# A feed-forward stage with a written-out order on every engine

## The chip, the cores and the metric

The kernel runs on one core of one Trainium2 chip. Its time is the device time of one launch in microseconds (us), the median of three runs. Beside it stands one profiled execution, from which all rows below come. The engines are TensorE (PE), VectorE (DVE), ScalarE (ACT), GpSimd (POOL) and SyncE (SP); SP issues nearly all DMAs here. SBUF is the on-chip memory, PSUM the eight banks into which matmuls accumulate.

## The reference

One layer on x of 1024 positions by 1024 channels, float32: pre-norm, one input projection, a convolution branch and a stick-breaking attention branch, a gated merge, an output projection, a post-norm added to the residual; then a dense feed-forward with 2816 hidden columns, post-normed and added again. The change lies in the last three lines and in the norms around them:

```python
h = rmsnorm(x, norm_ffn_pre)
gu = jnp.einsum('bsd,df->bsf', h, w_ffn_up)
gate, up = jnp.split(gu, 2, axis=-1)
ff = jnp.einsum('bsf,fd->bsd', jax.nn.silu(gate) * up, w_ffn_down)
x = x + rmsnorm(ff, norm_ffn_post)
```

## The kernel before

All products are float32 from three matmuls: an operand is split into a high part `wh` (a rounded copy, ACT) and a low part `wl` (the rest, a subtraction on POOL or DVE), and `mm3` (L74) adds high×high (L77), high×low (L78) and low×high (L80).

The feed-forward takes 2×2 blocks with seven products in place of eight. In the up phase, block f of 22 (`up`, L894) runs products 1, 2, 6, 5, 7, 3, 4, each 12 matmuls of 128x512 into one PSUM bank. Their weights come from two DMAs, `rg` (gate half) and `ru` (up half). `rg` split gives products 1 and 2 (`prep_a`); two DVE sums of `ru` and `rg` (`s`, L863, L864) give products 5 and 6; two more in place of `rg` (L865, L866) give 7 and 3; half of `ru` gives 4. DVE and ACT turn the banks into u2, u3, c11, c12, c22 and two activations a1, a2; on odd blocks POOL makes four sums `sa` of them. All are stored to DRAM. Product 4 multiplies with T4, made on DVE from T2 and B21 (`make_t4`, L883).

Beside this, `weight_sums` (L838) makes sums of the down weights: a tile `q` is loaded, four DVE operations of 128x256 run in place (L841 to L844), and the result is stored. `jobs` (L1023) says at which block each of the 22 is written down.

The down phase is 42 steps, six for each of seven products, in the order 1, 6, 7, 5, 4, 2, 3. `ready(n)` (L1002) splits the step's two operands, `ra` with POOL and `rb` with DVE, three steps ahead; `cell` (L1012) runs the matmuls into four banks; `evacuate` (L1104) empties them, and for products 4 and 3 also normalises, adds x1 and stores (`finish`, L1097).

Between the output projection and the up phase, `post(tb)` (L688) makes the residual x1 and the normed tile `xr` for 128 rows, and `operands(tb)` (L728) transposes and splits it. The first products, 1 and 2 of blocks 0 to 2, need only half of the rows and run early (L805 to L812).

A scheduler orders the instructions of each engine by its own costs, apart from those that `keep_in_program_order` pins (one use, L723). A tile waits for the readers of what lay in its place before. An engine takes its instructions strictly one after the other: one that waits holds those behind it.

Of the kernel before, what the change touches and what calls it, by code (L numbers as in the profile page):

```python
# [15 lines left out]
P = 128  # L16
# [21 lines left out]
def layer_kernel(ctx, tc, x, vecs, dww, gains, ident_d, mask_d, wv, wi, wbr, wo, wu, wdq, wd, out):  # L38
# [649 lines left out]
    def post(tb):  # L688
# [77 lines left out]
    for tb in range(2):  # L766
        post(tb)
    for tb in range(2, NT):
        pos_[tb] = [bank("po"), bank("po")]
        if tb < NT - 1:  # L770
            for e in range(2):
                out_steps(tb, e, range(NK), pos_[tb][e])
        else:
            for d in range(NK):
                for e in range(2):
                    out_steps(tb, e, [d], pos_[tb][e])
        operands(tb - 2)
        post(tb)

# [18 lines left out]
    for f in range(2):  # L798
        fetch_gate(f)
        prep_a(f)  # L800
    raw2 = op_.tile([P, 1024], F32, name="rg2", tag="wh", bufs=6)
    SP.dma_start(out=raw2, in_=wu[2])
    w2 = split(raw2, op_, tag="w", bufs=6)
    ops[2] = {1: (w2, 0), 2: (w2, HALF)}
    early[0] = [bank("m1"), bank("m2")]  # L805
    prod(early[0][0], *ops[0][1], B11)
    operands(NT - 2)
    prod(early[0][1], *ops[0][2], B21)
    for f in (1, 2):
# [3 lines left out]
    pin[0] = True  # L813
    operands(NT - 1)
# [9 lines left out]
    fp.tile([P, 4, 256], F32, name="q0", tag="q", bufs=2)  # L824
# [34 lines left out]
    def prep_s12(f):  # L859
        rg, ru = rgs[f], rus[f]  # L860
        s12 = fp.tile([P, 1024], F32, name="s12", tag="s", bufs=1)
        s1, s2 = s12[:, 0:HALF], s12[:, HALF:1024]
        V.tensor_tensor(out=s1, in0=ru[:, 0:HALF], in1=ru[:, HALF:1024], op=ALU.add)  # L863
        V.tensor_tensor(out=s2, in0=s1, in1=rg[:, 0:HALF], op=ALU.subtract)  # L864
        V.tensor_tensor(out=rg[:, 0:HALF], in0=rg[:, 0:HALF], in1=ru[:, 0:HALF], op=ALU.subtract)  # L865
        V.tensor_tensor(out=rg[:, HALF:1024], in0=rg[:, HALF:1024], in1=s2, op=ALU.subtract)  # L866
        w = split(s12, fp)
        ops[f][5], ops[f][6] = (w, 0), (w, HALF)

    def prep_s34(f):  # L870
# [12 lines left out]
    def make_t4():  # L883
        for k in range(4):
# [7 lines left out]
    quads = {}  # L892

    def up(f, mid):  # L894
        if f not in early:
            early[f] = [bank("m1")]
            product(f, 1, early[f][0])
        if len(early[f]) == 1:
            early[f].append(bank("m2"))
            product(f, 2, early[f][1])  # L900
# [6 lines left out]
        last = f == NFB - 1  # L907
        p6, p5, p7, p3, p4 = [None] * 5

        def run(i):  # L910
            ps = bank(f"m{i}")
            product(f, i, ps)
            return ps

        if last:
            p5, p3 = run(5), run(3)
            mid(0)
        p6 = run(6)
        V.tensor_tensor(out=u2, in0=p6, in1=u2, op=ALU.add)
        if not last:  # L920
            mid(0)
            p5 = run(5)
        mid(1)
        p7 = run(7)
        u3 = ev("u3")
        V.tensor_tensor(out=u3, in0=p7, in1=u2, op=ALU.add)
        up2 = half_tile("c22", "c", 3)
        V.tensor_tensor(out=up2, in0=p5, in1=u3, op=ALU.add)
        V.tensor_tensor(out=u2, in0=p5, in1=u2, op=ALU.add)
        if not last:  # L930
            p3 = run(3)
# [270 lines left out]
```

## Time and profile before

| | us |
|---|---|
| median of 3 runs | 1479.9 (1479.01 to 1481.78) |
| the profiled execution, its own time | 1481.82 |
| its span | 1479.8 |

The span is the time from the first to the last instruction that the profiler saw; about 2 us of the execution's time lie outside it. Mean granted TensorE clock over the span: 0.975 of full speed. PE is busy for 1381.4 us of the span. The output projection ends and the feed-forward begins at about 787 us; the up phase runs to 1256 us, the down phase to 1472 us.

### The profile page before, as it was taken

The page shows a single profiled execution, that of the slowest core. Times are in us where ns is not written, and L with a number is a line of the kernel's source. Part 1 is how long each engine was busy: PE and PEld are TensorE (multiplying, and loading weights), DVE is VectorE, ACT ScalarE, POOL GpSimd, SP SyncE. Part 2 cuts the span into 40 slices and gives each one's busy share as a digit, 9 for nine tenths or more (in the row PEclk, how much of TensorE's full clock was granted, in tenths as well). Part 3 has the DMA queues.
Part 4 walks back from the last instruction along what each step waited for, and adds up shares of the span by engine and source line. Part 5 has one row for each costly group of instructions (what it writes and reads, how often), then busy time and mean ns, then how long its engine had stood idle before and what let it go on. Part 6 is the DMA issues. An engine that isn't in the chain of part 4 may idle for free.

```text
span 1479.8 us, 17335 instructions
## 1 busy us (share of the span) xinstructions
PE 1381.4 (93%) x6412; PEld 1131.8 (76%) x6412; DVE 1021.7 (69%) x1221; ACT 528.0 (36%) x863; POOL 619.9 (42%) x465
## 2 busy tenths in 40 slices
PE   6988998998999879999997899899999999999997
PEld 5866787877888667887786677677888888788886
DVE  6498878776999996235347997787666543754583
ACT  5466655553102105132324312222333223443441
POOL 2233323332315232323205555544666654554672
PEclk9999999999999989999999899999999999999999
DMA  6011001101111110213322266654333334976552
GB/s 219 23 28 37 22 23 32 41 29 36 50 43 51 43 43 22 64 43 122 127 87 100 91 206 228 238 195 156 107 114 110 106 100 146 321 277 199 197 186 85
DMA packets 62403, 160.97 MB, mean 109 GB/s; under 512 B 6384, under 2 KB 17904, under 8 KB 62320
## 3 DMA queue, kind: packets, MB, share of 16 engines
q1 hardware_dynamic: 62320, 159.88, 32.9%
q8 instruction: 50, 0.82, 0.2%
q14 instruction: 33, 0.27, 0.1%
HBM read 117.65 MB, written 40.11 MB: 107 GB/s over the span
## 4 chain that ended last, share of the span: by engine, by line
PE 60%; DVE 24%; issue 7%; DMA 3%; POOL 3%; ACT 2%; SPq 0%; DVEq 0%; POOLq 0%; ACTq 0%
DVE acc L453 11%; PE m L77 7%; PE m L78 7%; PE m L80 7%; PE md L77 4%; PE md L78 4%; PE md L80 4%; PE pg L77 2%; PE pg L78 2%; PE pg L80 2%; POOL wl L787 2%; DVE R L260 2%; PE po L670 1%; PE po L669 1%; PE po L668 1%
## 5 line engine op out<-in xcount | busy, mean ns | idle before, releaser
L71 POOL TENSOR_TENSOR wl<-wraw,wh 128x1024 fp32r<-128x1024 f32 (+1 forms) x58 | 139.9, 2418 | 251.4 <-ACT wh L70 146.6
L453 DVE SCALAR_TENSOR_TENSOR acc<-u,dw,acc 128x1024 f32<-128x1024 f32 x120 | 177.0, 1532 | 0.3
L77 PE MATMUL m<-hH,wh 128*128 128x512 f32 x352 | 139.5, 396 | 0.0
L78 PE MATMUL m<-hL,wh 128*128 128x512 f32 x352 | 138.9, 395 | 0.0
L1008 POOL TENSOR_TENSOR wl<-ra,wh 128x1024 fp32r<-128x1024 f32 (+1 forms) x42 | 101.4, 2417 | 85.5 <-ACT wh L1007 78.5
L77 PE MATMUL m<-t,wh 128*128 128x512 f32 x264 | 108.2, 410 | 23.2 <-ACT wh L786 16.5
L1008 DVE TENSOR_TENSOR wl<-rb,wh 128x1024 fp32r<-128x1024 f32 (+1 forms) x42 | 90.5, 2163 | 55.0 <-ACT wh L1007 43.6
L77 PE MATMUL md<-wh 128*128 128x512 f32 x308 | 120.6, 394 | 3.4 <-ACT wh L1007 3.4
L78 PE MATMUL md<-wl,wh 128*128 128x512 f32 x308 | 120.8, 392 | 0.0
L787 POOL TENSOR_TENSOR wl<-rg,wh 128x1024 fp32r<-128x1024 f32 x44 | 110.0, 2500 | 25.3 <-ACT wh L786 22.7
L70 ACT ACTIVATE wh<-wraw 128x1024 fp32r<-128x1024 f32 (+1 forms) x60 | 56.5, 944 | 144.6 <-PE pg L78 50.7
L78 PE MATMUL m<-t,wh 128*128 128x512 f32 x264 | 107.1, 406 | 0.0
L77 PE MATMUL pg<-hH,wh 128*128 128x512 f32 x256 | 101.2, 395 | 0.0
L78 PE MATMUL pg<-hL,wh 128*128 128x512 f32 x256 | 99.7, 389 | 0.0
L80 PE MATMUL md<-wh,wl 128*128 128x512 f32 x308 | 97.5, 390 | 0.0
L80 PE MATMUL m<-hH,wl 128*128 128x512 f32 x352 | 95.6, 393 | 0.0
L863 DVE TENSOR_TENSOR s<-ru 128x512 f32<-128x512 f32 x22 | 39.1, 1778 | 72.6 <-POOL wl L787 72.6
L77 PEld LDWEIGHTS m<-t,wh 128*128 128x128 f32 x264 | 51.4, 195 | 39.0 <-ACT wh L786 18.5
L1007 ACT ACTIVATE wh<-ra 128x1024 fp32r<-128x1024 f32 (+1 forms) x42 | 41.5, 989 | 109.8 <-issue 73.8
L261 POOL TENSOR_TENSOR R<-sg,R 128x512 f32<-128x512 f32 x32 | 46.7, 1461 | 81.0 <-DVE R L260 77.6
L787 POOL TENSOR_TENSOR wl<-ru,wh 128x512 fp32r<-128x512 f32 x22 | 30.5, 1385 | 114.8 <-ACT wh L786 114.6
L77 PEld LDWEIGHTS m<-hH,wh 128*128 128x128 f32 x352 | 66.6, 189 | 15.5
(224 smaller groups left out, 3559.9 us busy)
## 6 DMA issues: line engine op xcount, KB each, us to landing
ra<-act SPq DMA_DIRECT2D x35, 512.0 KB, 4.7
wraw<-in_wi SPq DMA_DIRECT2D x32, 512.0 KB, 3.6
rg<-in_wu SPq DMA_DIRECT2D x23, 512.0 KB, 3.6
ru<-in_wu SPq DMA_DIRECT2D x22, 512.0 KB, 4.1
q<-in_wdq SPq DMA_DIRECT2D x22, 512.0 KB, 4.0
wsum<-q SPq DMA_DIRECT2D x22, 512.0 KB, 2.9
act<-sa SPq DMA_DIRECT2D x44, 256.0 KB, 2.6
rb<-wsum SPq DMA_DIRECT2D x20, 512.0 KB, 4.3
```

Of the source, the lines that this page charges most:

```text
L70: A.activation(out=wh, in_=raw, func=AF.Copy)
L71: (sub or G).tensor_tensor(out=wl, in0=raw, in1=wh.bitcast(F32), op=ALU.subtract)
L77: PE.matmul(ps, lhsT=lh, rhs=rh, start=(first and j == 0), stop=False)
L78: PE.matmul(ps, lhsT=lh, rhs=rl, start=False, stop=False)
L80: PE.matmul(ps, lhsT=ll, rhs=rh, start=False, stop=(last and j == n - 1))
L260: V.tensor_tensor_scan(out=R[:, 4:4 + n][:, ::-1], data0=d, data1=d, initial=carry, op0=ALU.mult, op1=ALU.bypass)
L261: G.tensor_tensor(out=R[:, 4:4 + n], in0=sg[:, 0:n], in1=R[:, 4:4 + n], op=ALU.mult)
L453: V.scalar_tensor_tensor(out=acc, in0=u[:, kk:kk + S], scalar=dw[:, cb, kk:kk + 1], in1=acc, op0=ALU.mult, op1=ALU.add)
L787: (low or G).tensor_tensor(out=wl, in0=src, in1=wh.bitcast(F32), op=ALU.subtract)
L863: V.tensor_tensor(out=s1, in0=ru[:, 0:HALF], in1=ru[:, HALF:1024], op=ALU.add)
L1007: A.activation(out=h, in_=src, func=AF.Copy)
L1008: eng.tensor_tensor(out=l, in0=src, in1=h.bitcast(F32), op=ALU.subtract)
```

## The change

`post(tb)` now comes before `operands(tb - 2)`, and the last two x1 stores are issued by ACT. The first gate weights are fetched inside the loop over tb. All six early products stand together, with the last `operands` between the last two. The pool of the up phase, "upp", sets the places of the tags c, ev, q, ch, cl first, so that `ru` and `s` come to lie elsewhere. The weight sums and splits are cut into four functions. From the up loop to the end all five engines are wrapped in `Ordered`, which pins every instruction to the written order. `weight_sums(f)` stands once in each block. Block 0 runs products 3, 5, 6, 7, 4, with `make_t4` between, and the last block the same without it. The stores of the result go through `late` and `flush`.

```diff
@@ post
         V.tensor_tensor(out=x1, in0=x1, in1=xt, op=ALU.add)
-        SP.dma_start(out=x1d[tsl, :], in_=x1)
+        if tb < NT - 2:
+            SP.dma_start(out=x1d[tsl, :], in_=x1)
...
+        if tb >= NT - 2:
+            A.dma_start(out=x1d[tsl, :], in_=x1)
@@ before the up loop
+        post(tb)
         operands(tb - 2)
-        post(tb)
...
+        if NT - 4 < tb < NT - 1:
+            f = tb - NT + 3
+            fetch_gate(f)
+            prep_a(f)
+    raw2, wh2, wl2 = [op_.tile([P, 1024], dt, name=nm, tag="wh", bufs=6) for nm, dt in (("rg2", F32), ("wh2", F32R), ("wl2", F32R))]
...
+    for f in range(3):
         early[f] = [bank("m1"), bank("m2")]
         prod(early[f][0], *ops[f][1], B11)
+        if f == 2:
+            pin[0] = True
+            operands(NT - 1)
         prod(early[f][1], *ops[f][2], B21)
...
-    fp.tile([P, 4, 256], F32, name="q0", tag="q", bufs=2)
+    for tag, w, n in (("c", HALF, 3), ("ev", HALF, 3), ("q", 1024, 2), ("ch", HALF, 1), ("cl", HALF, 1)):
+        fp.tile([P, w], F32, name=f"{tag}0", tag=tag, bufs=n)
@@ up
+    class Ordered:
...
+        def __getattr__(self, nm):
+            fn = getattr(self.eng, nm)
+            return lambda *a, **k: tc.keep_in_program_order(fn(*a, **k))
...
+        if 2 < nf < NFB:
+            prep_a(nf)
         u2 = ev("u2")
         A.activation(out=u2, in_=p1, func=AF.Copy)
+        if more and f:
+            sums_12(nf)
...
+        if f == 0 or last:
+            run(3)
+            run(5)
+            if f == 0:
+                make_t4(range(4))
+                sums_12(nf)
+            run(6)
+            after_6()
+        else:
+            run(6)
+            after_6()
+            run(5)
+        weight_sums(f)
+        if more:
+            split_12(nf)
+        run(7)
...
+        if more:
+            sums_34(nf)
...
+        if more:
+            split_34(nf)
+        run(4)
+        if more:
+            prep_c(nf)
@@ the up loop
-    jobs = [[] for _ in range(NFB)]
-    for n in range(NFB):
-        jobs[min(1 + n if n < 10 else n, NFB - 2)].append(n)
...
+    PE, V, A, G, SP = [Ordered(e) for e in (PE, V, A, G, SP)]
     for f in range(NFB):
...
+        up(f)
@@ finish
-            SP.dma_start(out=out[tb * P:(tb + 1) * P, es], in_=parts[e])
+            late.append((out[tb * P:(tb + 1) * P, es], parts[e]))
```

What this does to the queues is shown at three places. In these rows L910 stands for every pinned instruction, since all are issued from that line.

The first is DVE at the start of the up phase, before the change: `da`, `db` and `t` are T4, `s` and `rg` the sums of block 0's weights.

```order
L886 TENSOR_TENSOR da<-t_5787,hH 128x512
L887 TENSOR_TENSOR db<-t_5787,hL 128x512
L886 TENSOR_TENSOR da<-t_5787,hH 128x512
L888 TENSOR_TENSOR da<-da,db 128x512
L887 TENSOR_TENSOR db<-t_5787,hL 128x512
L886 TENSOR_TENSOR da<-t_5787,hH 128x512
L863 TENSOR_TENSOR s_6717<-ru 128x512
L890 TENSOR_TENSOR t_6660<-da,t_6660 128x512
L864 TENSOR_TENSOR s_6717<-s_6717,rg 128x512
```

And after it, at the same place (`c_6742` is c11 of block 0):

```order
L867 TENSOR_TENSOR s_6721<-ru 128x512
L868 TENSOR_TENSOR s_6721<-s_6721,rg 128x512
L872 TENSOR_TENSOR rg<-rg,ru 128x512
L873 TENSOR_TENSOR rg<-rg,s_6721 128x512
L910 TENSOR_TENSOR c_6742<-m_6553,u_6740 128x512
L910 TENSOR_TENSOR da<-t_5787,hH 128x512
L910 TENSOR_TENSOR db<-t_5787,hL 128x512
```

The sums of block 0 moved ahead of T4. Further along the same queue T4 ends so (`s_6805` are the sums of block 1, `u_6740` is u2 of block 0, which empties its product 6):

```order
L910 TENSOR_TENSOR t_6660<-da,t_6660 128x512
L910 TENSOR_TENSOR s_6805<-ru 128x512
L910 TENSOR_TENSOR s_6805<-s_6805,rg 128x512
L910 TENSOR_TENSOR u_6740<-m_6808,u_6740 128x512
L910 TENSOR_TENSOR q<-q 128x256 x4
```

All 16 operations of T4 and the first two sums of block 1 now stand ahead of the operation that empties block 0's product 6, and one `weight_sums`, the four operations on `q`, behind it.

The second place is SP at the end of the output projection, before the change. Of the names, `x1d` is the store of the residual, `rg_6521` the gate weights of block 2, `ru` the up weights of blocks 0 and 1.

```order
L691 DMA xr<-in_x 128x1024
L802 DMA rg_6521<-in_wu 128x1024
L702 DMA x1d<-x_6395 128x1024
L702 DMA x1d<-x_6491 128x1024
L857 DMA ru<-in_wu 128x1024 x2
```

The two stores of x1 stand ahead of `ru`. After the change:

```order
L691 DMA xr<-in_x 128x1024
L806 DMA rg_6521<-in_wu 128x1024
L861 DMA ru<-in_wu 128x1024 x2
L840 DMA q<-in_wdq 128x1024
L910 DMA rg<-in_wu 128x1024
```

The two stores left SP's queue. The first `ru` now takes the place of `wl2`, the low part of block 2's gate weights, and so waits for the last matmul of block 2's product 2; before, it took a place that `xr` of the last 128 rows held.

The third is DVE at the end of the down phase's product 4, where `wl<-rb` is a split for a step to come, `du<-du,md` empties a bank, and the operations with `pr` and `x1r` finish a tile of the result. Before:

```order
L1118 TENSOR_TENSOR du_10001<-du_10001,md 128x512
L1118 TENSOR_TENSOR du_10002<-du_10002,md 128x512
L1008 TENSOR_TENSOR wl<-rb,wh 128x1024
L103 TENSOR_SCALAR pv<-ss_10013 128x1
L1118 TENSOR_TENSOR du_10003<-du_10003,md 128x512
L1101 SCALAR_TENSOR_TENSOR du_10001<-du_10001,pr,x1r 128x512
```

A split stands between the second and the third bank. After:

```order
L910 TENSOR_TENSOR du_10005<-du_10005,md 128x512
L910 TENSOR_SCALAR pv<-ss_10017 128x1
L910 SCALAR_TENSOR_TENSOR du_10005<-du_10005,pr,x1r 128x512
L910 SCALAR_TENSOR_TENSOR dc_10009<-dc_10009,pr,x1r 128x512
L910 TENSOR_TENSOR du_10006<-du_10006,md 128x512
L910 TENSOR_SCALAR pv<-ss_10018 128x1
```

The four tiles are now finished one after the other, and the next split stands behind the last of them (16 rows in all).

## Rows read from the trace of the kernel before

**Rows 1.** The page: busy us, share of the span, instructions.

```profile
PE 1381.4 (93%) x6412; PEld 1131.8 (76%) x6412; DVE 1021.7 (69%) x1221; ACT 528.0 (36%) x863; POOL 619.9 (42%) x465
```

**Rows 2.** PE's waits by releaser, 787 to 1475 us: total, times, longest.

```profile
PE m L77 <- ACT wh L786: 16.5, 3, 12.3
PE m L77 <- DVE u L926: 6.4, 4, 2.5
PE m L80 <- POOL wl L787: 4.1, 4, 3.1
PE md L77 <- ACT wh L1007: 3.4, 1, 3.4
PE tp L721 <- DVE xr L706: 0.9, 1, 0.9
```

**Rows 3.** Stretches of the span: each engine's busy us and instructions, clock, DMA share.

```profile
core 0: us, PE busy (x) PEld busy (x) DVE busy (x) ACT busy (x) POOL busy (x), PEclk, DMA share, GB/s
...
830.00:884.00 54.00, 50.57 (x210) 40.16 (x209) 49.39 (x62) 14.61 (x20) 30.82 (x15) 0.97 0.50 162
884.00:1020.00 136.00, 124.46 (x508) 97.87 (x508) 109.87 (x146) 31.42 (x43) 69.53 (x36) 0.96 0.62 214
1020.00:1256.00 236.00, 236.00 (x1023) 191.92 (x1022) 129.88 (x162) 67.17 (x89) 137.99 (x73) 1.00 0.36 115
```

**Rows 4.** Tile q in two of these: VectorE's busy us and operations, clock, DMA.

```profile
884.00:1020.00 136.00, 50.67 (x70) 0.96 0.62 214
1020.00:1256.00 236.00, 0.26 (x1) 1.00 0.36 115
```

**Rows 5.** PE timeline at the gap: start, us, instruction, idle before.

```profile
819.33 0.80 PE L77 MATMUL m<-t,wh 128*128 128x512 f32 x1 [12.30 <-ACT wh L786]
...
820.36 0.63 PE L77 MATMUL m<-t,wh 128*128 128x512 f32 x1
820.78 0.63 PE L78 MATMUL m<-t,wh 128*128 128x512 f32 x1
```

**Rows 6.** SP timeline, 803 to 806 us.

```profile
803.66 0.81 SPq L857 DMA_DIRECT2D ru<-in_wu  x2
```

**Rows 7.** DMA issues: count, KB each, us to landing.

```profile
ru<-in_wu SPq DMA_DIRECT2D x22, 512.0 KB, 4.1
...
x1r<-x1d SPq DMA_DIRECT2D x8, 512.0 KB, 4.9
```

**Rows 8.** DVE timeline, 810 to 819 us.

```profile
815.24 0.68 DVE L863 TENSOR_TENSOR s<-ru 128x512 f32<-128x512 f32 x1
...
817.51 0.68 DVE L864 TENSOR_TENSOR s<-s,rg 128x512 f32<-128x512 f32 x1
```

**Rows 9.** ACT timeline, 814 to 819 us.

```profile
814.21 0.63 ACT L889 ACTIVATE t<-da 128x512 fp32r<-128x512 f32 x1 [3.02 <-DVE da L888]
...
818.22 1.06 ACT L786 ACTIVATE wh<-s 128x1024 fp32r<-128x1024 f32 x1 [2.87 <-DVE s L864]
```

**Rows 10.** POOL timeline, 815 to 823 us.

```profile
815.49 1.55 POOL L787 TENSOR_TENSOR wl<-ru,wh 128x512 fp32r<-128x512 f32 x1 [3.12 <-ACT wh L786]
819.36 2.88 POOL L787 TENSOR_TENSOR wl<-s,wh 128x1024 fp32r<-128x1024 f32 x1 [2.32 <-ACT wh L786]
```

**Rows 11.** DVE timeline, 844 to 850 us.

```profile
844.92 0.42 DVE L844 TENSOR_TENSOR q<-q 128x256 f32<-128x256 f32 x1
...
846.19 2.60 DVE L842 TENSOR_TENSOR q<-q 128x256 f32<-128x256 f32 x1
```

**Rows 12.** POOL timeline, 846 to 849 us.

```profile
846.09 2.42 POOL L787 TENSOR_TENSOR wl<-rg,wh 128x1024 fp32r<-128x1024 f32 x1 [1.73 <-ACT wh L786]
```

**Rows 13.** DVE timeline in the down phase, 1416 to 1417 us.

```profile
1416.21 1.77 DVE L1101 SCALAR_TENSOR_TENSOR du<-du,pr,x1r 128x512 f32<-128x512 f32 x1 [2.23 <-POOL pr L105]
```

**Rows 14.** DVE timeline of the last tile, from 1472 us.

```profile
1472.11 0.69 DVE L1128 TENSOR_TENSOR du<-md,du 128x512 f32<-128x512 f32 x1 [3.08 <-PE md L80]
...
1475.80 0.75 DVE L1101 SCALAR_TENSOR_TENSOR du<-du,pr,x1r 128x512 f32<-128x512 f32 x1
```

More of the change, by code (lines that the diff above doesn't have):

```diff
@@ L881, in product, with make_t4 @@
         prod(ps, w, c0, OPERAND[i], first, last)
-    def make_t4():
-        for k in range(4):
+    def make_t4(ks):
+        for k in ks:
             da, db = half_tile("da", "a", 8), half_tile("db", "a", 8)
@@ L890, in make_t4, with __init__, up @@
             V.tensor_tensor(out=T4[1][:, k, :], in0=da, in1=T4[0][:, k, :].bitcast(F32), op=ALU.subtract)
-    quads = {}
-    def up(f, mid):
-        if f not in early:
[L896 to L900, printed above, removed]
+    quads, s12s = {}, {}
+    class Ordered:
+        def __init__(self, eng):
+            self.eng = eng
+        def __getattr__(self, nm):
+            fn = getattr(self.eng, nm)
+            return lambda *a, **k: tc.keep_in_program_order(fn(*a, **k))
+    def up(f):
+        nf = f + 1
+        more, last = nf < NFB, f == NFB - 1
+        if f not in early:
+            early[f] = [bank("m1"), bank("m2")]
+            for i in (1, 2):
+                product(f, i, early[f][i - 1])
         p1, p2 = early[f]
+        if 2 < nf < NFB:
+            prep_a(nf)
         u2 = ev("u2")
         A.activation(out=u2, in_=p1, func=AF.Copy)
+        if more and f:
+            sums_12(nf)
         gate1 = half_tile("c11", "c", 3)
@@ L906, in up, with after_6 @@
         A.activation(out=gate1, in_=gate1, func=AF.Silu)
-        last = f == NFB - 1
-        p6, p5, p7, p3, p4 = [None] * 5
-        def run(i):
[L911 to L924, printed above, removed]
+        flush()
+        if last:
+            fetch(0)
+        else:
+            if f + 2 < NFB:
+                fetch_gate(f + 2)
+                fetch_up(f + 2)
+            fetch_q(nf)
+        ps = {}
+        def run(i):
+            ps[i] = bank(f"m{i}")
+            product(f, i, ps[i])
+        def after_6():
+            V.tensor_tensor(out=u2, in0=ps[6], in1=u2, op=ALU.add)
+        if f == 0 or last:
[6 more added lines that the diff above has]
+            after_6()
+        else:
+            run(6)
[5 more added lines that the diff above has]
+        run(7)
         u3 = ev("u3")
-        V.tensor_tensor(out=u3, in0=p7, in1=u2, op=ALU.add)
+        V.tensor_tensor(out=u3, in0=ps[7], in1=u2, op=ALU.add)
         up2 = half_tile("c22", "c", 3)
[L928 to L931, printed above, removed]
+        V.tensor_tensor(out=up2, in0=ps[5], in1=u3, op=ALU.add)
+        V.tensor_tensor(out=u2, in0=ps[5], in1=u2, op=ALU.add)
+        if more:
+            sums_34(nf)
+        else:
+            ready(0)
+        if 3 not in ps:
+            run(3)
         gate2 = half_tile("c12", "c", 3)
-        V.tensor_tensor(out=gate2, in0=p3, in1=u2, op=ALU.add)
+        V.tensor_tensor(out=gate2, in0=ps[3], in1=u2, op=ALU.add)
         A.activation(out=gate2, in_=gate2, func=AF.Silu)
@@ L967, in layer_kernel @@
         fetch_up(1)
-    prep_s12(0)
-    prep_s34(0)
+        sums_12(0)
+        split_12(0)
+        sums_34(0)
+        split_34(0)
+    fetch_q(0)
     prep_c(0)
-    make_t4()
     NSETS = 6
@@ L1150, in layer_kernel @@
         evacuate(order[-1], p, banks[p])
+        flush()
     tctx.close()
```

83 lines of the change are left out of this document (24 added, 59 removed).

## The prediction

> **What bounds the kernel now.** The page comes first: PE is busy for 1381.4 of 1479.8 us, no other engine for more than 69% [rows 1]. So time is to be had only where PE stands or runs slowly. The list of PE's waits over the feed-forward says for what: 16.5 us for ScalarE copies (one of them 12.3), 6.4 for VectorE operations that empty a bank, 4.1 for GpSimd splits, 3.4 at the start of the down phase, 0.9 for a transpose [rows 2]. The table of stretches then says where. From 1020 to 1256 us PE never idles: 1023 matmuls in 236.0 us, 0.2307 us each, granted clock 1.00. From 884 to 1020 the same work takes 136 us for 508 matmuls [rows 3]; at 0.2307 they would take 117.2. So 18.8 us are lost there, in idle time and in a clock of 0.96.
>
> What differs between the two stretches is the tile q: 70 of its operations lie in the first, costing VectorE 50.7 us, and one in the second [rows 4]. VectorE is busy for 109.9 of 136 us in the first, for 129.9 of 236 in the second [rows 3]. A block of 84 matmuls lasts 84 x 0.2307 = 19.4 us, so 884 to 1020 holds about six blocks, and 70 / 4 = 17.5 weight sums, three to a block. The scheduler took all 22 as early as it could. One such operation takes 0.42 us alone and 2.60 when it starts beside a GpSimd split that began just before it and lasts 2.42 [rows 11, 12]. What empties a bank stands behind them.
>
> **The start, part by part.** PE ends its transposes at 807.03 and stands for 12.30 us until 819.33 (its next start less the idle time) [rows 5]. `ru` was issued at 803.66 [rows 6] and lands in 4.1 us [rows 7], at 807.8, but the sum that reads it runs at 815.24 and the next at 817.51, since T4's operations stand in front and between; the ScalarE copy of 1.06 us at 818.22 ends the wait [rows 8, 9].
>
> In the new order the residual's norm comes before the transposes, so the wait of 0.9 us [rows 2] goes: -0.9, and PE ends its early work at 807.03 - 0.9 = 806.1. But the first `ru` now waits for PE's last early matmul, so it is issued 2.4 us later than before and lands at 806.1 + 4.1 = 810.2. Then nothing stands in front: four sums of 0.68 (2.7), one copy of 1.06, first product at 814.0. The wait is 7.8 us in place of 12.3: -4.5. If the transfer is slower or the sums are held beside a split, as much as 2.9 us is lost per hold [rows 10], so the term lies between 0 and -6.
>
> Product 3, now first, needs the low part that is third in GpSimd's queue. The half split of `ru` (1.55) starts at 810.9, the split of `s` (2.88) ends at 815.5, that of `rg`, as long, at 818.4 [rows 10]. Eight matmuls lie ahead of its use; after the gap they come 0.42 apart [rows 5], the lower of the clock's two levels, 1.2 GHz, so they cover 3.4 us from 814.0: wait 1.0 (0 to 3): +1.1 with rounding up. The slow clock itself is lost in both kernels.
>
> T4 now stands whole in front of what empties product 6 of block 0, and product 4 waits for that. A quarter of T4 is three VectorE operations of 0.68, one ScalarE copy of 0.63 [rows 9], one more of 0.68: 3.35, four of them 13.4. The first operations fall beside the splits that end at 815.5 and 818.4, so I let T4 start in effect at 816.5: it ends at 829.9, the two sums of block 1 and the emptying add 2.0: 831.9. PE comes there at 814.0 + 48 x 0.2307 + 1.0 + 1.8 (slow clock) = 827.9. Wait 4.0, bounds 0 (T4 starts at once, one quarter overlaps the other's copy) and 7 (three more holds of one operation); with the clock's fall I take 4.5. VectorE and GpSimd enter blocks 1 to 3 late by about this, with one weight sum each on top: product 6 of block 1 stands behind the first of them, product 1 of block 3 behind GpSimd's four `sa` sums. No row shows these waits; between 0 and 6 I take 2.6.
>
> What goes: the longest of the GpSimd waits, 3.1 [rows 2], falls into this stretch, among the weight sums, and the clock of 0.97 over 54 us [rows 3] is 1.6 more; with a short wait beside them -5.0. The range is 0 to -5.
>
> **The blocks.** With one weight sum per block, VectorE has 129.9 / (236 / 19.4) = 10.7 us of other work per block and 4 x 50.7 / 70 = 2.9 of q: 13.6 of 19.4. Read along the written order, the splits of the next block's weights are ready at least 5 us before PE needs them, and each bank has a whole block to be emptied. So I expect 0.2307 in blocks 4 to 21 as in the late blocks of before: -18.8; the range is -9 (half the stalls stay) to -21. What would be late next is the split for block f+1's first product, which has the most of a block as its cover.
>
> **The down phase.** The start stays: the second VectorE split for it stands behind the last block's operations, as the waits of 3.4 show [rows 2]; 0 (-3.4 to +4). At the end of product 4 four tiles are now finished one after the other. The last tile's chain, from emptying to the end of the second scaling, is 1472.11 to 1476.55, 4.44 us [rows 14]; here GpSimd multiplies and VectorE waits 2.23 for it [rows 13], so about 5. Four make 20, and the next step's split, 2.2 to 2.4, stands behind. The chain starts 2 us before the step ends, so the split is done 20.3 us after; the three steps already split are 72 matmuls, 16.6 us. Wait 0 to 6; I take 2.5 and 1.0 of slower clock: +3.5.
>
> The tail: the fetch of x1 for the last tile now stands behind the stores of the tile before, which go out about 4.4 us into the last 33 matmuls (7.6 us). It lands 4.9 later [rows 7], at 9.3, and is needed 3.0 after them, at 10.6: hidden by 1.3 us. 0 to +2, taken 0. Stores of x1 issued by ScalarE: no row has one; two issues on SP take 0.81 [rows 6], ScalarE idles 3.02 just then [rows 9], SP held nothing that was needed: taken 0, between -0.8 and 0.8.
>
> **Sum.** -0.9 - 4.5 + 1.1 + 4.5 + 2.6 - 5.0 - 18.8 + 3.5 = -17.5. The profiled execution took 1481.8, 1.9 above the median of 1479.9 and at the upper end of the three; 1481.8 - 17.5 = 1464.3, which I put at 1464.
>
> **Rivals.**
> *VectorE becomes the bound in every block* (slower). Ten of its operations in a block read SBUF alone (four sums, four of q, two products); each can be held as in [rows 11]. GpSimd works 138.0 / 12.2 = 11.3 us per block [rows 3]; if VectorE stood through half of that beyond what it does now, it would need 13.6 + 5.7 = 19.3, which only just fits, and through all of it 24.9, 5.5 too much, in 18 blocks 99 us. From 19.4 + 17.5 / 18 = 20.4 us per block on, the kernel is slower. A middle price of 2.7 a block gives 1464 + 49 = 1513. For it: the rows of q, and that a bank's emptying can't pass them now. Against: in the late blocks the six others ran beside GpSimd without one PE wait. The Trainium skill ("SBUF — State Buffer", section "SBUF: two separate sides") has the two engines share a port pair that one holds for a whole instruction, while the other stands; the trace agrees with 2.60 beside 2.42, and by that rule the two have 11.3 us and 6 x 0.68 + 4 x 0.42 = 5.8 us to place in 19.4, which would still fit. Chance 0.07.
> *The start eats the gain.* The gap stays 12.3 because `ru` leaves later, and T4 and blocks 1 to 3 cost twice my terms: 17.5 - 4.5 - 7.1 = 5.9 gained, 1476. For it: `ru` does leave later. Against: its sums now run at once. Chance 0.10.
> *Half the stalls of the weight sums stay*, spread over 22 blocks: 1464 + 9.4 = 1474. Chance 0.06; against it is VectorE's slack of 5.8 us per block.
> *None of the new waits comes* (T4, blocks 1 to 3, product 4): 1464 - 10.6 = 1453. Chance 0.12.
>
> **How the numbers follow.** The forecast has 0.65, with 1456 to 1472 as its own range from its bounds. For 8 in 10 the range takes in the better case and most of the two smaller gains: 1447 to 1478. About 3 us, 0.2%, is what a measurement can tell. Of the cases at 1474 and 1476 some fall within it or beyond; so faster 0.87, the same 0.04, slower 0.09.
>
> **What would show it.** Right: PE's first product after the early ones 8 us after them; a wait of some 4 us in front of block 0's last product; q spread evenly, four operations per 19.4 us, and no PE wait from the fifth block to the last; matmuls of the down phase beginning near 1235 us; a short wait three steps after product 4. Wrong: a PE wait for a VectorE or GpSimd operation that comes again in every block; a gap of 12 us at the start; a tail longer than the 7.7 us that now lie between the emptying of the last bank at 1472.11 [rows 14] and the end of the span at 1479.8.

## The result: 0.7% slower, and where the time went

| | median us | ratio to the kernel before, 95% interval |
|---|---|---|
| before, run beside it | 1479.68 | |
| changed | 1491.34 (1489.14 to 1491.93) | 1.0074 [1.0056, 1.0091] |

The forecast was 1464 us, with a range of 1447 to 1478. The profiled execution of the changed kernel took 1491.46 us, its span 1489.7, at a mean granted clock of 0.976; before, span 1479.8 at 0.975. All times here are of executions at clocks of 0.97 to 0.99; one of the kernel below that finishes product 4 later took 2270.5 us at a clock of 0.558 and is left out (with it, that kernel's median would be 1485.4).

From the start of PE's first matmul of each phase, and the start of the last one of the down phase:

| us | before | changed | difference | forecast |
|---|---|---|---|---|
| first product of the up phase | 787.4 | 786.1 | -1.3 | 0 |
| length of the up phase | 468.6 | 457.7 | -10.9 | -21.0 |
| length of the down phase | 215.7 | 238.0 | +22.3 | +3.5 |
| from its end to the end of the span | 8.1 | 7.9 | -0.2 | 0 |

The forecast's -0.9, a wait of a transpose, stands in the up phase: before, it lay 4 us behind the first product. The -1.3 of the first row says little, since each profile is of one execution: among the kernels below with the same code up to that point it lies between 783.5 and 789.0. The lengths of the phases repeat better (the up phase of the eight profiles in which it is pinned throughout and written as here: 457.6 to 458.5) and carry the argument.

The page of the changed kernel: busy us, share of the span, instructions.

```profile
PE 1381.4 (93%) x6412; PEld 1128.6 (76%) x6412; DVE 1135.0 (76%) x1221; ACT 526.0 (35%) x863; POOL 639.2 (43%) x465
```

PE and the instruction counts are as in [rows 1], but VectorE is busy 113 us longer with the same 1221 instructions. PE's waits, 787 to 1490 us, beside [rows 2]:

```profile
PE md L910 <- DVE wl L910: 15.8, 4, 6.9
PE m L910 <- ACT wh L775: 8.6, 1, 8.6
PE m L910 <- DVE u L910: 5.2, 1, 5.2
PE m L910 <- ACT wh L910: 4.5, 2, 4.2
PE md L910 <- POOL wl L910: 2.1, 3, 1.3
```

The gap of 12.3 became 8.6, the waits for the operations that empty a bank (`u`) are gone from the blocks but for one, and in their place the down phase (`md`) waits 15.8 us for VectorE splits. The stretches, beside [rows 3], and VectorE's work on tile q in two of them, beside [rows 4]:

```profile
830.00:884.00 54.00, 50.69 (x206) 40.11 (x207) 51.07 (x51) 13.87 (x19) 31.16 (x15) 0.94 0.40 138
884.00:1020.00 136.00, 136.00 (x588) 109.76 (x587) 128.83 (x123) 36.66 (x51) 84.60 (x42) 1.00 0.42 150
1020.00:1220.00 200.00, 200.00 (x862) 161.09 (x860) 189.83 (x173) 51.84 (x71) 128.29 (x63) 1.00 0.45 157
1244.00:1482.00 238.00, 218.57 (x924) 177.03 (x923) 144.36 (x103) 88.48 (x117) 125.71 (x60) 0.96 0.58 200
```
```profile
884.00:1020.00 136.00, 38.65 (x29) 1.00 0.42 150
1020.00:1220.00 200.00, 62.52 (x43) 1.00 0.45 157
```

Between 884 and 1020 PE is now busy throughout, 588 matmuls in place of 508: the stalls are gone. But VectorE is busy for 189.83 of 200 us, 95%, where the forecast had 13.6 of 19.4, 70%. An operation on q takes 62.52 / 43 = 1.45 us there. The down phase runs at a clock of 0.96 (before, 0.99 from 1256 to 1472).

Where PE stands in the changed kernel (start, us, instruction, idle before it and its releaser):

```profile
812.38 0.79 PE L910 MATMUL m<-hH,wh 128*128 128x512 f32 x1 [8.61 <-ACT wh L775]
...
831.01 3.75 PE L910 MATMUL m<-t,wh 128*128 128x512 f32 x8 [5.22 <-DVE u L910]
...
1228.33 0.69 PE L910 MATMUL m<-hH,wh 128*128 128x512 f32 x1 [4.20 <-ACT wh L910]
...
1246.14 0.50 PE L910 MATMUL md<-wl,wh 128*128 128x512 f32 x1 [1.96 <-DVE wl L910]
...
1257.28 0.80 PE L910 MATMUL md<-wl,wh 128*128 128x512 f32 x1 [5.41 <-DVE wl L910]
...
1427.96 0.79 PE L910 MATMUL md<-wl,wh 128*128 128x512 f32 x1 [6.89 <-DVE wl L910]
1428.55 0.63 PE L910 MATMUL md<-wh 128*128 128x512 f32 x1
1428.98 0.63 PE L910 MATMUL md<-wl,wh 128*128 128x512 f32 x1
...
1449.77 0.50 PE L910 MATMUL md<-wh 128*128 128x512 f32 x1 [1.54 <-ACT wh L910]
1451.77 0.50 PE L910 MATMUL md<-wl,wh 128*128 128x512 f32 x1 [1.50 <-DVE wl L910]
```

Behind the long waits matmuls come 0.43 us apart for a while, as from 1428.55 to 1428.98, the lower of the clock's two levels (1.2 GHz); after the 6.89 that costs another 2.55. A loss is counted below as the time beyond so many matmuls at their even distance, so it holds both. It is 10.3 us at the start of the down phase (5.5 before), 9.6 after product 4, and 7.5 in the last product (0.2 before); by another choice of the even distance the last figure, and those like it below, are up to 0.6 larger.

The third long wait is the last block's product 3. It now comes first in that block, and its sums come late on VectorE:

```profile
1215.05 7.90 DVE L910 TENSOR_TENSOR q<-q 128x256 f32<-128x256 f32 x4
...
1225.38 0.68 DVE L910 TENSOR_TENSOR rg<-rg,s 128x512 f32<-128x512 f32 x1
```

One weight sum took 7.90 us, not 2.9, and the sums, the ScalarE copy of 1.04 at 1227.24 and so the product stand behind it. Nearly all that time GpSimd is at work, at two of its sums `sa` and then at two splits, of which this is the first:

```profile
1217.54 2.58 POOL L910 TENSOR_TENSOR wl<-rg,wh 128x1024 fp32r<-128x1024 f32 x1
```

GpSimd makes `sa` sums for every second block only; in the blocks between, the four operations take about half:

```profile
1041.88 3.87 DVE L910 TENSOR_TENSOR q<-q 128x256 f32<-128x256 f32 x4
```

VectorE at the end of product 4, beside [rows 13]; it is the written order that the third place of the change shows:

```profile
1402.45 0.69 DVE L910 TENSOR_TENSOR du<-du,md 128x512 f32<-128x512 f32 x1 [4.91 <-PE md L910]
1403.99 0.21 DVE L910 TENSOR_SCALAR pv<-ss 128x1 f32<-128x1 f32 x1 [0.85 <-ACT junk L910]
1405.87 0.75 DVE L910 SCALAR_TENSOR_TENSOR du<-du,pr,x1r 128x512 f32<-128x512 f32 x1 [1.67 <-POOL pr L910]
...
1407.21 0.68 DVE L910 TENSOR_TENSOR du<-du,md 128x512 f32<-128x512 f32 x1
...
1420.10 2.86 DVE L910 SCALAR_TENSOR_TENSOR du<-du,pr,x1r 128x512 f32<-128x512 f32 x1 [1.67 <-POOL pr L910]
1422.88 2.82 DVE L910 SCALAR_TENSOR_TENSOR dc<-dc,pr,x1r 128x512 f32<-128x512 f32 x1
1425.62 2.28 DVE L910 TENSOR_TENSOR wl<-rb,wh 128x1024 fp32r<-128x1024 f32 x1
```

Each of the first three chains lasts 4.7 to 4.8 us, of which VectorE stands 0.85 + 1.67 waiting for ScalarE and GpSimd. The two scalings of the fourth take 2.8 in place of 0.75, since GpSimd's own splits begin just ahead of them:

```profile
1420.03 6.79 POOL L910 TENSOR_TENSOR wl<-ra,wh 128x1024 fp32r<-128x1024 f32 x3
```

The split that PE needs stands behind all of it.

### The profile page after: what moved, and what is told of

Read it like the earlier page. It is cut to its first block, busy times and chain, and to the rows that moved or that the text cites. A ratio compares the mean times of both kernels' runs of the same rounds, so it can differ in the third digit from the quotient of the medians.

```text
span 1489.7 us, 17351 instructions
## 1 busy us (share of the span) xinstructions
PE 1381.4 (93%) x6412; PEld 1128.6 (76%) x6412; DVE 1135.0 (76%) x1221; ACT 526.0 (35%) x863; POOL 639.2 (43%) x465
## 4 chain that ended last, share of the span: by engine, by line
PE 56%; DVE 27%; issue 7%; POOL 3%; DMA 3%; ACT 2%; SPq 0%; DVEq 0%; POOLq 0%; ACTq 0%
PE m L910 18%; PE md L910 11%; DVE acc L453 11%; DVE q L910 3%; PE pg L77 2%; PE pg L78 2%; PE pg L80 2%; DVE R L260 2%; DVE R L255 1%; PE po L670 1%; PE po L669 1%; PE po L668 1%; DVE aL L321 1%; POOL wl L910 1%; PE av L291 1%
## 5 line engine op out<-in xcount | busy, mean ns | idle before, releaser
L910 POOL TENSOR_TENSOR wl<-rg,wh 128x1024 fp32r<-128x1024 f32 x40 | 101.8, 2545 | 120.2 <-ACT wh L910 120.2
L910 PE MATMUL m<-hH,wh 128*128 128x512 f32 x328 | 131.7, 401 | 12.8 <-ACT wh L775 8.6
L910 POOL TENSOR_TENSOR wl<-ra,wh 128x1024 fp32r<-128x1024 f32 (+1 forms) x42 | 109.6, 2626 | 70.8 <-ACT wh L910 70.3
L910 PE MATMUL m<-t,wh 128*128 128x512 f32 x528 | 134.6, 397 | 5.5 <-DVE u L910 5.2
L910 PE MATMUL md<-wl,wh 128*128 128x512 f32 x308 | 123.0, 399 | 15.8 <-DVE wl L910 15.8
L910 ACT ACTIVATE c<-c 128x512 f32<-128x512 f32 x44 | 27.8, 633 | 303.4 <-DVE c L910 303.4
L910 PE MATMUL m<-hL,wh 128*128 128x512 f32 x328 | 130.8, 399 | 0.0
L910 DVE TENSOR_TENSOR wl<-rb,wh 128x1024 fp32r<-128x1024 f32 (+1 forms) x42 | 99.9, 2417 | 40.2 <-ACT wh L910 23.0
L910 DVE TENSOR_TENSOR q<-q 128x256 f32<-128x256 f32 x88 | 123.1, 1399 | 2.3
L910 PE MATMUL md<-wh 128*128 128x512 f32 x308 | 122.6, 398 | 1.5 <-ACT wh L910 1.5
L910 PEld LDWEIGHTS m<-t,wh 128*128 128x128 f32 x528 | 100.0, 190 | 29.7 <-issue 5.6
L910 PE MATMUL md<-wh,wl 128*128 128x512 f32 x308 | 99.9, 399 | 2.1 <-POOL wl L910 2.1
L910 PE MATMUL m<-hH,wl 128*128 128x512 f32 x328 | 90.6, 398 | 2.1 <-POOL wl L910 1.7
L910 PEld LDWEIGHTS m<-hH,wh 128*128 128x128 f32 x328 | 62.6, 191 | 28.4 <-ACT wh L775 9.0
L910 PEld LDWEIGHTS md<-wl,wh 128*128 128x128 f32 x308 | 59.4, 193 | 30.3 <-DVE wl L910 17.5
L910 PEld LDWEIGHTS m<-hH,wl 128*128 128x128 f32 x328 | 60.9, 188 | 19.8 <-POOL wl L910 5.4
```

What stands on the lines that cost most here:

```text
L910: return lambda *a, **k: tc.keep_in_program_order(fn(*a, **k))
```

## The experiments

### What the pins cost in the down phase

The theory after the result: the written order removes the stalls in the blocks, and pinning the down phase costs more than that. First all pins were taken out:

```diff
-    PE, V, A, G, SP = [Ordered(e) for e in (PE, V, A, G, SP)]
```

> No pins at all from the up loop on; the code is written as in the changed kernel, one weight sum per block, but the scheduler orders it. Theory A (the pins are what spreads the weight sums; the scheduler takes them early again): some 20 us of waits and slow clock between 840 and 1020 us as before the change, time 1477 to 1482. Rival C (one weight sum per block in the code is enough, pins or not): no PE wait in the middle of the up phase, time 1465 to 1470, like the kernel that is pinned in the up loop alone.

Measured: 1472.8 us, 0.9949 [0.9934, 0.9964]. Its waits of PE from 800 us:

```profile
PE m L77 <- ACT wh L775: 13.1, 2, 10.9
PE m L77 <- DVE u L963: 6.6, 5, 2.5
PE m L77 <- DVE u L944: 5.0, 1, 5.0
PE md L77 <- ACT wh L1052: 3.3, 1, 3.3
```

The down phase takes 215.7 us again, with one wait of 3.3 and no loss after product 4 or in the last product. The stalls between 884 and 1020 are back: 527 matmuls there, and 56 operations on q. All else in the change is worth 0.5% faster. VectorE's order here shows how nothing comes to be lost after product 4:

```profile
1416.18 2.89 DVE L1115 SCALAR_TENSOR_TENSOR dc<-dc,pr,x1r 128x512 f32<-128x512 f32 x1
1419.00 3.44 DVE L1053 TENSOR_TENSOR wl<-rb,wh 128x1024 fp32r<-128x1024 f32 x1
1422.36 2.88 DVE L1115 SCALAR_TENSOR_TENSOR du<-du,pr,x1r 128x512 f32<-128x512 f32 x1
```

The scheduler puts splits between and inside the chains. Scalings are held 2.9 us here too, and nothing waits for them.

Then the pins in the up loop alone, and in the down phase alone (all five engines are pinned from behind the up loop):

```diff
+    plain = PE, V, A, G, SP
     PE, V, A, G, SP = [Ordered(e) for e in (PE, V, A, G, SP)]
     for f in range(NFB):
         up(f)
+    PE, V, A, G, SP = plain
```

> The engines are pinned to the written order in the up loop alone; the down phase is ordered by the scheduler again, all else as in the changed kernel. Theory A (the written order of the down phase costs the 22 us by which that phase became longer, 216 to 238 us from its first matmul to its last): down phase 216 to 219 us, time 1467 to 1471. Rival B (the stores of the result through late and flush, or the later weight sums, hold the down phase back, and not the pins): down phase over 230 us, time 1484 to 1491.

> The changed kernel with the up loop ordered by the scheduler and all engines pinned from the end of that loop on. Theory A (the pins cost in the down phase by themselves): the 9 us wait with its slow clock after product 4 and the 7.5 us at the last product come as in the changed kernel, 15 to 20 us above the kernel without pins (1472.8), 1488 to 1493. Rival (they come from the hand-over of a pinned up phase): 1473 to 1478.

Up loop alone: 1480.74 us, 1.001 [1.000, 1.002], between the two expectations: the waits of the second half of the down phase are gone, but its start still waits 1.91 and 7.00 (length 223.7). Down phase alone: 1494.02 us, 1.0092 [1.0076, 1.0107], its length 235.0. Against the kernel without pins that is +19.3 us in length and +21 in the medians, and these are the longest waits in its down phase:

```profile
PE md L910 <- DVE wl L910: 13.3, 3, 6.9
PE md L910 <- ACT wh L910: 2.7, 1, 2.7
```

So the pins of the down phase cost 19.3 us by themselves, behind an up phase without pins; behind the pinned one they cost 14.3 (238.0 against 223.7). The difference lies in the start of the down phase: it loses 5.5 us without any pins, 6.7 with the down phase alone pinned, but 13.4 with the up loop alone pinned and 10.3 with both. The costs that follow the pins are those after product 4 and in the last product.

### Which part of the pinned down phase

All engines pinned, but product 4's tiles finished one in each later step, behind that step's `ready`, which also needs four places for the tile `x1r` in place of two:

```diff
-        xt = dp.tile([P, D], F32, name="x1r", tag="x1r", bufs=2)
+        xt = dp.tile([P, D], F32, name="x1r", tag="x1r", bufs=4)
...
-            finish(p + 4, (c21[p], c22[p]), sst2[p], xt)
+            put_off.append((p + 4, (c21[p], c22[p]), sst2[p], xt))
...
             ready(n + AHEAD)
+        if put_off:
+            finish(*put_off.pop(0))
```

> All pinned as in the changed kernel, but the four tiles of the down phase's product 4 are finished one per later step, each behind that step's splits, and x1r has four places. Theory A (VectorE stood for four chains of 4.7 us with the next split behind them): the wait of 6.9 us three steps after product 4 and its slow clock (2.6) go, and some of the 7.5 us at the last product, time 1475 to 1482. Rival D (SP's queue, held by the stores of the result, brings the operands late): the waits stay within 3 us of what they are, time 1488 to 1492.

Measured: 1484.48 us, 1.0035 [1.0021, 1.0048]. The wait of 6.9 is gone and the down phase falls from 238.0 to 228.2. The four chains were that wait; that the places of `x1r` were not is read from the rows above, where VectorE's scalings wait for `pr` and none for `x1r`. The last product still loses 8.9 us. Two edits on top of it (product 2's squares, on ScalarE, and the multiplications with the gains, on GpSimd, behind the last splits; with that, splits four steps ahead), and one of SyncE's queue behind the up loop of the changed kernel, looked for why:

```diff
-            square(0, c11[p], sst1[p])
-            gained(0, c11[p], G)
+            behind.append(p)
...
+    for p in behind:
+        square(0, c11[p], sst1[p])
+        gained(0, c11[p], G)
     for p in range(4):
```
```diff
-        if n + AHEAD < N:
+        if n < 33:
             ready(n + AHEAD)
+        elif n == 33:
+            ready(36)
+            ready(37)
+        elif n + 4 < N:
+            ready(n + 4)
```
```diff
+    sp_plain = SP
     PE, V, A, G, SP = [Ordered(e) for e in (PE, V, A, G, SP)]
...
+    SP = sp_plain
```

> All pinned, product 4 finished one tile per later step as in the kernel before it in this study (1485.4), and besides the squares (ScalarE) and gains (GpSimd) of product 2 stand behind the last three splits in place of ahead of them. Theory A (those eight operations held the splits of the last product's fourth step): the 9 us lost there fall to under 3, time 1476 to 1480. Rival (the operands themselves come late over SP's queue): the loss stays, time 1483 to 1487.

> All pinned, product 4 finished later and product 2's squares and gains behind, as in the last pinned kernel (1483.8), and from step 33 on each step's operands are split four steps ahead in place of three, so that the split of the fourth step of the last product stands ahead of the emptying of product 2. Theory A (the last product needs all six steps' splits within its first 33 matmuls, and the pinned queue holds three of them behind product 2's emptying): the 6.7 us lost at the last product fall to under 3, time 1477 to 1481. Rival (the operands land late): 1483 to 1487.

> The changed kernel with SP alone ordered by the scheduler from the end of the up loop on; PE, VectorE, ScalarE and GpSimd stay pinned. Theory A (two costs: VectorE's four chains after product 4, and, at the last product, operands fetched late because SP's pinned queue holds the fetches behind stores of the result that wait for those chains): the 6.9 us wait stays, the 7.5 us at the last product fall to under 3, time 1483 to 1487. Rival (the last product waits for its splits behind product 2's emptying on VectorE and ScalarE, SP has no part): time 1489 to 1492.

Product 2's squares later: 1483.79 us, 1.0026 [1.0015, 1.0037], the last product loses 6.7. Splits four steps ahead as well: 1483.14, 1.0015 [1.0004, 1.0027], loss 8.0; ScalarE now waits for operands, 9.48 us once; on SyncE their fetches stand behind stores. SyncE free in the down phase of the changed kernel: 1494.09, 1.0103 [1.0081, 1.0125], with the waits of 6.91 and of the last product as before. So SyncE's order is not what costs the last product its time in the changed kernel, and the squares and gains are a small part: with them out of the way 8.9 fell to 6.7. Two more runs joined these: the first edit with SyncE free, and the second with SyncE free and operands fetched six steps ahead from step 27:

```diff
-        if n + AHEAD + 2 < N:
-            fetch(n + AHEAD + 2)
+        if n < 27:
+            fetch(n + 5)
+        elif n == 27:
+            fetch(32)
+            fetch(33)
+        elif n + 6 < N:
+            fetch(n + 6)
```

> Product 4 finished one tile per later step, product 2's squares and gains behind (the kernel at 1483.8), and SP free in the down phase as well. Theory A: both costs are gone, under 2 us lost from the third step of the down phase to its end, time 1475 to 1478. Rival (as for the kernel before): the loss of 6.7 us at the last product stays, 1482 to 1485.

> All queues pinned, except SyncE's in the down phase, which takes its transfers as their places come free; the down phase's operands are fetched six steps ahead from step 27 and split four steps ahead from step 33, so that in VectorE's list only the splits of steps 40 and 41 stand behind the emptying of product 2; product 4 is finished one tile per later step and product 2's squares come after the last splits. Theory A (the last product loses its time since the splits of its later steps stand behind product 2's emptying in VectorE's list): the last product loses under 3 us beyond its steady pace, the time is 1476 to 1480 us. Rival (VectorE, whose scalings are held some 2.9 us each beside GpSimd's sums, has no time there, in whatever order its list stands): the loss stays at 6 to 7 us and the time at 1482 to 1485 us.

Measured: 1483.19, 1.0034 [1.0021, 1.0046], loss 6.7; and 1482.05, 1.0025 [1.0011, 1.0038], loss 5.1. The last fell between the two theories. Its splits stand as in the run that lost 8.0; what differs is SyncE's free order and the earlier fetches, so about 3 us of that loss went with operands that came late. Against the run with SyncE free that lost 6.7, splits and fetches sooner are worth 1.6. One long wait stayed, for the first split of this row:

```profile
1432.35 2.87 DVE L910 SCALAR_TENSOR_TENSOR du<-du,pr,x1r 128x512 f32<-128x512 f32 x1 [0.66 <-POOL pr L910]
1435.14 2.90 DVE L910 SCALAR_TENSOR_TENSOR dc<-dc,pr,x1r 128x512 f32<-128x512 f32 x1
1437.96 4.51 DVE L910 TENSOR_TENSOR wl<-rb,wh 128x1024 fp32r<-128x1024 f32 x2
```

The fourth chain with its two held scalings stands in front of it. VectorE had idled 4.87, 3.03 and 2.68 us between 1400 and 1415 at other waits of its list, so it did not lack time as such. How much of the last product's loss in the changed kernel is order and how much is holding stays open.

### The up phase

The last block in the order of the others:

```diff
-        if f == 0 or last:
+        if f == 0:
```

> The last block runs its products 6, 5, 7, 3, 4 like the others, where the changed kernel runs 3 and 5 first. Theory A (product 3 of the last block comes before its weights are split in the written order, which costs 4.2 us of wait and 1.7 of slower clock at 1224 us): no wait there, time 1485 to 1486. Rival (running 3 and 5 first is what covers the first splits of the down phase): the wait moves to the start of the down phase, which loses 5 us more than the 10 it loses now, time 1490 to 1492.

Measured: 1487.28 us, 1.0053 [1.0037, 1.0069]. The wait of 4.20 is gone, but the start of the down phase now has waits of 2.02, 2.06 and 3.88, where the changed kernel has 1.96 and 5.41. Part of the gain moved there.

All five engines pinned in blocks 0 to 19 only, and the same with the last quarter of T4 behind the emptying of product 6:

```diff
+        if f == 20:
+            PE, V, A, G, SP = plain
```
```diff
-                make_t4(range(4))
-                sums_12(nf)
+                make_t4(range(3))
             run(6)
             after_6()
+            if f == 0:
+                make_t4(range(3, 4))
+                sums_12(nf)
```

> The engines are pinned in blocks 0 to 19 alone; blocks 20 and 21 and the down phase are ordered by the scheduler. Theory A (the pins pay in the blocks where the weight sums are, and cost where the last block begins, at the hand-over to the down phase and in that phase): no PE wait between 880 us and the down phase, the wait of 4.2 us before block 21 gone, 3 to 6 us lost at the start of the down phase as before the change, time 1462 to 1467. Rival (a pinned queue handed to the scheduler brings the first operands of the down phase late, as in the kernel pinned in the up loop alone, which lost 12 us there): time 1470 to 1476.

> As the kernel pinned in blocks 0 to 19, and T4 is cut in the written order: three quarters ahead of the operation that empties block 0's product 6, the last quarter and the sums of block 1 behind it. Theory A (that operation stood behind T4 and held the bank of product 4 for 5.2 us): the wait falls to under 2 us, time 4 to 6 us below the kernel pinned in blocks 0 to 19, 1457 to 1463. Rival (VectorE's work is what bounds the first blocks, so the wait only moves into block 1): within 2 us of that kernel.

Measured: 1476.91, 0.9978 [0.9965, 0.9992], and 1476.97, 0.9982 [0.9968, 0.9996]. The down phase still takes 224.9 in the first. In the second 0.87 us of the T4 wait stay in front of block 0's product 4, and 4.46 moved on into block 1: T4 is VectorE's work, and at both places it delays what stands behind.

Then the pins of single engines in blocks 0 to 19: VectorE alone; all but VectorE; and VectorE alone with block 0 in its old order and T4 ahead of the loop.

```diff
-    PE, V, A, G, SP = [Ordered(e) for e in (PE, V, A, G, SP)]
+    V = Ordered(V)
```
```diff
-    PE, V, A, G, SP = [Ordered(e) for e in (PE, V, A, G, SP)]
+    PE, A, G, SP = [Ordered(e) for e in (PE, A, G, SP)]
```
```diff
     prep_c(0)
+    make_t4(range(4))
...
-        if f == 0 or last:
+        if last:
```

> As the kernel pinned in blocks 0 to 19, but VectorE alone is pinned. Theory A (what mattered was where the weight sums stand in VectorE's queue): no PE wait over 1 us between 880 and 1200 us, time within 3 us of the kernel with all five engines pinned there. Rival (the order on ScalarE, GpSimd and SP, the splits and the fetches, does the work): waits come back between 900 and 1010 us, time 1468 to 1480.

> The changed kernel with PE, ScalarE, GpSimd and SP pinned in blocks 0 to 19, VectorE and all that follows ordered by the scheduler. Theory A (VectorE's order is the gain): waits between 880 and 1020 us as without pins, 1472 to 1480. Rival (SP's pinned fetches alone keep the weight sums one per block, since a sum can't run before its tile is loaded): no such waits, time within 3 us of the kernel pinned on all engines in blocks 0 to 19 (1476.9) and q spread evenly over the up phase.

> VectorE pinned in blocks 0 to 19 (the kernel at 1468.8), with block 0 as before the change: products 6, 5, 7, 3, 4, T4 ahead of the loop and not pinned. Theory A (the new order of the first block costs what separates 1468.8 from the 1458.5 of the kernel before with VectorE pinned: T4 whole in front of a bank's emptying): a gap of 10 to 13 us at the start but no 5 us wait before product 4 and none in block 1, time 1459 to 1464. Rival (the other places of ru and s, with ru behind PE's last early matmul, cost it): 1466 to 1470.

VectorE alone: 1468.78 us, 0.9927 [0.9907, 0.9948]; no wait from 861 to 1235. All but VectorE: 1511.79, 1.0212 [1.0197, 1.0227], slower than anything else, with this at the head of PE's waits:

```profile
PE m L910 <- ACT wh L910: 20.4, 10, 2.5
PE m L910 <- ACT wh L775: 12.5, 1, 12.5
```

Neither theory had foreseen it: the q operations are spread, yet a copy comes late in every second block. One of them, at 1004.70 us, stands on ScalarE behind an activation that waited 7.35 us for VectorE: a queue with a written order, behind an engine that does not keep to it. With the old block 0: 1464.13, 0.9902 [0.9886, 0.9917]; the gap is 9.7, and of the wait of 5.0 in front of product 4 there is nothing left. The new order of the first block costs about 4.6 us: the up phase takes 449.9 us with it and 445.3 without, and the medians lie as far apart, though the intervals of the two ratios overlap.

Last, the kernel before with two things alone: `jobs` holds one weight sum per block (block 20 has two and block 21 none), and VectorE is pinned in blocks 0 to 19.

```diff
-    jobs = [[] for _ in range(NFB)]
-    for n in range(NFB):
-        jobs[min(1 + n if n < 10 else n, NFB - 2)].append(n)
+    jobs = [[min(f, NFB - 2)] if f < NFB - 2 else [NFB - 2, NFB - 1] if f == NFB - 2 else [] for f in range(NFB)]
...
+    plain, V = V, Ordered(V)
...
+        if f == 20:
+            V = plain
         up(f, mid)
```

> The kernel before the change with one part of it alone: one weight sum per block, and VectorE pinned to the written order in blocks 0 to 19; places, start, products and down phase as before. Theory A (VectorE's order is the gain): no PE wait between 900 and 1020 us, the 12.3 us gap at the start stays, 13 to 18 us under the kernel before less up to 6 us at the start of the down phase, time 1463 to 1472. Rival (the gain needs the new product order and the places too): time 1475 to 1480.

Measured: 1458.51 us, 0.9844 [0.9826, 0.9861], the fastest of all, faster than both kernels. All waits of PE from 800 us on, and two stretches:

```profile
PE m L77 <- ACT wh L786: 12.3, 1, 12.3
PE md L77 <- ACT wh L1007: 7.1, 1, 7.1
PE md L78 <- DVE wl L1008: 0.8, 1, 0.8
```
```profile
884.00:1020.00 136.00, 136.00 (x590) 110.56 (x589) 108.53 (x124) 40.08 (x50) 84.56 (x44) 1.00 0.50 166
1020.00:1220.00 200.00, 200.00 (x868) 162.51 (x867) 153.07 (x176) 57.21 (x72) 116.62 (x60) 1.00 0.45 154
```

The up phase takes 444.8 us, 23.8 less than before, which is the forecast's 18.8 + 5.0. One weight sum per block without the pin was run only in the changed kernel, where the stalls came back. VectorE is busy for 77% of the second stretch, not 95%: in the old order of a block its operations stand less often beside GpSimd's. A weight sum takes 2.89 us in one block and 5.82 in the next, where GpSimd makes its `sa` sums, against 3.87 and 7.90 in the changed kernel:

```profile
1015.38 2.89 DVE L1029 TENSOR_TENSOR q<-q 128x256 f32<-128x256 f32 x4
...
1034.79 5.82 DVE L1029 TENSOR_TENSOR q<-q 128x256 f32<-128x256 f32 x4
```

## Why the prediction was wrong, step by step

*Transposes and gap*: right. The wait of 0.9 is gone, the gap is 8.6 us (7.8 forecast), `ru` was issued at 803.83 just behind PE's last early matmul, and ScalarE's copy ends the gap.

*The low part for product 3*: 0.4 in place of 1.0. *T4*: right in mechanism; the wait is 5.2 (4.0), and it sits in front of block 0's product 4. By the count of losses above block 0 lost 8.0 us more than before, where 5.6 were forecast for these two. *Blocks 1 to 3*: three waits of 0.2, 0.4 and 1.7 between 855 and 869; with what went of the old waits these blocks lose 2.6 us less than before (2.6 - 5.0 = -2.4 forecast).

*The blocks*: right that the stalls go. No idle time of PE from 870 to 1224 in the changed kernel, and the runs with VectorE alone pinned, set against the one with no pins, show the order of that one queue to be the cause. Wrong was VectorE's slack: 13.6 us per block were forecast from 0.72 us for an operation on q and 10.7 of other work; it took 18.4 (189.83 / 200 of 19.4), since the weight sum, and other operations with it, stand where GpSimd works. The first rival, VectorE as the bound, gave 19.3 as the point that only just fits: it came that close, and no nearer. In the middle blocks the error cost little: in every second one a weight load waits 0.36 us for GpSimd's split, which "at least 5 us before PE needs them" had not foreseen, and blocks 4 to 20 lose 1.9 us by it.

*The last block* was not worked out at all. That the splits are ready "at least 5 us before PE needs them" does not hold where the order changes: product 3, the sixth of seven elsewhere, comes third there, and its sums stood behind a weight sum of 7.9 us. That cost 4.2 us and 1.65 of slow clock; the run in which that block has the order of the others shows it: its up phase has no such wait.

*The down phase* is the step that failed: "Wait 0 to 6; I take 2.5 and 1.0 of slower clock: +3.5". The mechanism named, four chains of about 5 us (4.7) with the split behind them, is what happened, as shown by the run that finishes later. It was too small, 6.9 + 2.6, and the two scalings beside GpSimd's splits, some 2 us each, were not put in. And it was the only one counted. The last product was not worked out, though the written order replaced the scheduler's there too, and lost 7.5 us; that the pins cause this loss is shown, by which of their orders is open. The start's extra 4.8 (10.3 against 5.5) was put at nothing as well ("The start stays", with bounds of -3.4 and +4). The Trainium skill ("SBUF — State Buffer", section "SBUF: two separate sides") has VectorE's operations with two SBUF inputs and GpSimd's take turns at a shared port pair, a whole instruction each; the trace agrees, with 2.86 against 0.75 beside a split that began 0.07 us earlier. The prediction used it for the blocks and not for the chains.

*The start of the down phase* loses more behind an up phase with pinned queues, whether the down phase is pinned or not: 8.6 to 14.6 in all such kernels, 5.4 to 6.7 in the three without. Its longest wait is 7.1 in the fastest kernel, which loses 10.3 there like the changed one, and 7.2 with VectorE alone pinned, against 3.4 before. So the extra 4.8 is for the most part not a cost of the pins of the down phase. Nor is it the price of a shorter up phase: with all but VectorE pinned that phase takes 494.9 us, and the start still loses 12.0. With VectorE alone pinned, the fetch that this wait is for follows the last stores of the up phase on SyncE:

```profile
1251.10 0.32 SPq L835 DMA_DIRECT2D act<-a  x1
1251.47 2.02 SPq L835 DMA_DIRECT2D act<-sa  x4
...
1255.57 0.42 SPq L1044 DMA_DIRECT2D ra<-act  x1
```
```profile
1263.52 1.06 ACT L1052 ACTIVATE wh<-ra 128x1024 fp32r<-128x1024 f32 x1 [9.64 <-DMA ra<-act]
```

It landed at 1263.45, and the ScalarE copy of it ends PE's wait at 1265.58. Whether an earlier fetch would shorten the wait, and whether stores or places hold it back, was not tried.

In sum: the up phase gained 10.9 of 21.0; of the missing 10.1 the last block took about 6, block 0 2.4 and blocks 4 to 20 1.9. The down phase cost 22.3 in place of 3.5; together with -1.3 and -0.2 that is the 9.9 us between the two spans.

## What to carry to other kernels

Pin the queue whose order was shown to be wrong, in the stretch where it is, and leave the rest to the scheduler: in the changed kernel five engines pinned to the end lost 0.7%, five engines in 20 blocks gained 0.2% and VectorE alone in these blocks gained 0.7%; in the kernel before, with its own order of a block and one weight sum in each, VectorE alone gained 1.6%. Whoever replaces a scheduler's order in a whole phase must follow each engine through every wait of that phase, the first and last iteration above all, and there count as its time also the waits inside a chain, which hold all that stands behind. Pinning the others while VectorE was free was the worst of all, +2.1%.

## What was not expected of the hardware

The same four operations on q took 2.89 and 5.82 us by turns in one order and 3.87 and 7.90 in another; over 200 us VectorE's busy time went from 153 to 190 with about the same number of operations, and only 15 of these 37 us are in q (47.23 against 62.52). A busy share is thus no property of the work alone, but also of what the neighbour does at that moment. PE ran 862 matmuls in 200 us in the changed kernel and 868 in the fastest, with no idle time of PE in either. In the changed kernel a wait shows on the weight loads (PEld) instead, five times in these 200 us:

```profile
1063.96 0.76 PEld L910 LDWEIGHTS m<-hH,wl 128*128 128x128 f32 x4 [0.36 <-POOL wl L910]
```

Each time two matmuls start 0.1 us later than the even distance has them, which is 1 us in all and so most of the difference; the fastest kernel has no such wait. A stretch in which PE never idles can still be slowed by an operand that comes just too late.
